# Copying queries and gates to the rounded type before their transposes, in both attention stages

## The chip, the cores and the metric

The kernel runs on one core of one Trainium2 chip. The metric is the device time of one execution in microseconds, and the kernel before takes 2444.26 us (median of three runs, 2442.14 to 2445.91). A core has five engines that the text speaks of: TensorE (PE in the profile, with its weight loads as PEld), VectorE (DVE), ScalarE (ACT), GpSimd (POOL) and SyncE (SP). SyncE only issues DMAs here; each engine works through its own instructions in order, and semaphores tie the engines together.

## The reference

One encoder layer is applied to two sequences of 2048 tokens with model width 1024. It normalises the input, projects it, attends in two head groups side by side, gates each group's output, projects back and adds a second gated input:

```
h = rms_norm(x);  proj = h @ w_in
q_a, k_a, v_a, g_a, q_b, k_b, v_b, g_b = split(proj)     # 512,128,128,512, 4 x 512
q_a, k_a: per-head rms_norm, partial rotary;  q_b, k_b: per-head rms_norm
o_a = windowed_gqa_sink(q_a, k_a, v_a, sink) * silu(g_a)  # 8 query heads, 2 kv heads, +-128 tokens
o_b = neighbourhood_attn(q_b, k_b, v_b, rpb) * silu(g_b)  # 8 heads, 2-D window on a grid 64 wide
x = x + concat(o_a, o_b) @ w_out
y = x + (p @ w_ple) * sigmoid(x @ w_ple_gate)
```

Everything is float32. The kernel keeps that precision with a rounded type (float32r, F32R in the code): a value is split into a rounded high part and the remainder, and each product is made of three products of rounded parts.

## The kernel before

**Stages.** The kernel goes through 96 blocks of 128 tokens, f = 0 to 95. The first 32 (two sequences of 16) are group A, where a block has two units, one for each kv head. The next 64 are group B, two halves of the heads with 32 blocks each, where a block is one unit. A last stage makes the output projections. In the attention stages the projections run ahead of the attention work of a unit as a stream of matmuls 512 columns wide, and the attention work of a unit is set into this stream at hand-written places: PLAN_A, PLAN_L (last unit of A), PLAN_B and PLAN_C are lists of (place in the unit, whether it is this unit's work or the previous unit's, action, index). The actions are scores (sc), exponentials (exp), in A the denominators (den), the transposes of the probabilities (pt), their products with the values (po), the preparation of the next block's queries (prep) and the end of the unit (fin). TensorE's order is pinned to the order in which the code emits its instructions (`pinned`); the other engines are ordered by the tile framework from dependencies and emission order, except where `P`, `behind` or `after` fixes a place.

**Transposes.** `tr` (lines 291 to 295) transposes a tile of 128 x 128 on TensorE with an identity: line 293 if the tile is of the rounded type, line 295 if it is plain float32. In group A's inner blocks, `turn` (line 736) copies a pair of probability tiles by a DMA on SyncE's queue, bits unchanged, to a tile of the rounded type, a ring of three places of 640 columns (`tna`), and line 293 transposes the copies. In the first and the last block of each sequence the probabilities are not copied and line 295 transposes them. In most of group B's units (`copied_`) the probabilities are copied in the same way by DMAs on ScalarE's queue (line 342).

**Queries.** In A, `prep_a` takes the block's queries (tile `qg`, 128 tokens by 8 heads of 64) from `held`, transposes them in a run of four as float32 into `pqt`, and `split_q` makes the high and low parts. In B, `prep_b` does so in a run of two into `pqtb`.

**Gates.** `exps` ends with GpSimd's product of the gate with the inverse denominators (line 359) into the tile `g2`, 256 columns, two buffers. `fin`, in the following unit, transposes it in a run of two as float32 into `pgt` or `pgtb`; VectorE multiplies it with the attention output (lines 809 and 1025), and SyncE stores the product (lines 810 and 1026).

**SyncE's queue** also carries the loads of inputs (`stx`, `stn`, line 393), the stores and loads of B's values (`v_d`, `vw`, lines 887 and 961), the bias loads (line 927) and the loads and stores of split weights (`wa`, `wb`, `sp_...`).

Of the kernel before, what the change touches and what calls it, by code (L numbers as in the profile page):

```python
# [11 lines left out]
F32 = mybir.dt.float32  # L12
F32R = mybir.dt.float32r
# [6 lines left out]
NT = SEQ // 128  # L20
KT = DM // 128
HD = 64
# [36 lines left out]
def bias_offsets():  # L59
# [32 lines left out]
KB = 23  # L92
PLAN_A = (
    (0.04, 1, "sc", 0), (0.08, 1, "sc", 1), (0.11, 1, "sc", 2), (0.12, 1, "rest", 0), (0.14, 1, "sc", 3),
    (0.14, 1, "rest", 1), (0.21, 0, "pt", 0), (0.26, 0, "pt", 1), (0.31, 0, "pt", 2),
    (0.32, 1, "exp", 0), (0.33, 1, "turn", 0), (0.33, 1, "turn", 1),
    (0.48, 0, "po", 0), (0.56, 0, "po", 1), (0.66, 1, "prep", 0), (0.66, 0, "po", 2), (0.74, 0, "fin", 0), (0.76, 1, "den", 0),
)
PLAN_L = tuple((part, now or act == "pt", act, i) for part, now, act, i in PLAN_A if act != "pt") + (
    (0.75, 1, "pt", 0), (0.79, 1, "pt", 1), (0.88, 1, "pt", 2),  # L100
# [1 line left out]
PLAN_B = (  # L102
    (0.00, 1, "sc", 0), (0.03, 1, "sc", 1), (0.07, 1, "sc", 2), (0.09, 0, "po", 2), (0.11, 1, "sc", 3), (0.16, 0, "po", 3),
    (0.16, 1, "exp", 0), (0.24, 0, "fin", 0), (0.35, 1, "prep", 0),
    (0.45, 1, "pt", 0), (0.52, 1, "pt", 1), (0.60, 1, "pt", 2), (0.66, 1, "po", 0), (0.74, 1, "pt", 3), (0.80, 1, "po", 1),
)
PLAN_C = (
    (0.00, 1, "sc", 0), (0.01, 0, "po", 0), (0.03, 1, "sc", 1), (0.05, 0, "po", 1), (0.07, 1, "sc", 2), (0.09, 0, "po", 2),
    (0.11, 1, "sc", 3), (0.16, 0, "po", 3), (0.16, 1, "exp", 0), (0.24, 0, "fin", 0), (0.35, 1, "prep", 0),
    (0.64, 1, "pt", 0), (0.73, 1, "pt", 1), (0.82, 1, "pt", 2), (0.91, 1, "pt", 3),  # L110
)


# [15 lines left out]
def emit(ctx, tc, io):  # L129
    nc = tc.nc  # L130
# [191 lines left out]
    def exps(sm, fct, gs, sink=None, turned=None):  # L322

        mx, nm, den, rd, ss = (sm[k] for k in ("mx", "nm", "den", "rd", "s"))
        if sink is None:
            nc.vector.tensor_scalar_mul(nm, mx, -1.0)  # L326
            yield
        else:
            nc.vector.scalar_tensor_tensor(out=nm, in0=mx, scalar=-1.0, in1=sink[1], op0=ALU.mult, op1=ALU.min)
            yield  # L330
        waiting = []
        for n_, i in enumerate((0, 2, 1, 3) if sink is None else range(4)):
            ex = nc.scalar.activation(ss[i], ss[i], AF.Exp, bias=nm[:, i:i + 1], accum_out=den[:, i:i + 1])  # L333
# [24 lines left out]
        g2 = ap.tile([128, 4, HD], F32, tag="g2", name="g2", bufs=2)  # L358
        nc.gpsimd.tensor_tensor(out=g2, in0=gs.rearrange("p (h d) -> p h d", h=4),
                                in1=rd.unsqueeze(2).broadcast_to([128, 4, HD]), op=ALU.mult)  # L360
        sm["g2"] = g2.rearrange("p h d -> p (h d)")
        yield

    def split_q(pqt, q1, q2, part):

# [339 lines left out]
    qrest = {}  # L705

    def prep_a(f):
        q = held[f][0]
        pqt = ptile([128, 512], "ms", "pqt")
        halves = pqt.rearrange("p (r x e q) -> p r e x q", r=2, x=2, e=2)  # L710
        for i in range(4):
            tr(halves[:, i // 2, i % 2], q[:, 2 * i:2 * i + 2, :].rearrange("p h d -> p (h d)"),
               ident.rearrange("p (x q) -> p x q", x=2))
        q1 = [ap.tile([128, 512], F32R, tag="q1", name="q1", bufs=3) for _ in range(2)]
        q2 = [q2s[f % 2][:, e] for e in range(2)]
        drain(split_q(pqt, q1, q2, 0))
        qrest[f] = split_q(pqt, q1, q2, 1)
        return q1, q2

    p_rot, s2, tn = [], [0, 0], []  # L720

    def unit_a(f, kv):
        s, t = divmod(f, NT)
# [5 lines left out]
        def turn(pair):  # L729

            if left and right:
                if len(s2) < 3:
                    s2.append(ap.tile([128, 3, 640], F32R, tag="ev", name="tna", bufs=1))
                to = s2[2][:, s2[1] % 3]
                s2[1] += 1
                nc.sync.dma_start(to.bitcast(F32), pairs[pair])
                pairs[pair] = to

# [57 lines left out]
        def fin(_):  # L796
# [9 lines left out]
            for e in range(2):  # L806
# [2 lines left out]
            nc.vector.tensor_tensor(out=ot, in0=pgt, in1=ot, op=ALU.mult)  # L809
            nc.sync.dma_start(oa_d[s].rearrange("(i p) q -> p i q", p=128)[:, 2 * kv:2 * kv + 2, 128 * t:128 * t + 128],  # L810
                              ot)
        return {"sc": sc, "turn": turn, "pt": pt, "po": po, "fin": fin, "prep": lambda _: nxt(f) if kv else None,
                "exp": lambda _: next(got["ex"]), "den": lambda _: next(got["ex"]), "rest": lambda _: None if kv else next(qrest[f])}

    pending = []
# [118 lines left out]
    def unit_b(f):  # L934
# [84 lines left out]
        def fin(_):  # L1019
            pgt = ptile([128, 2, 128], "sc", "pgtb")  # L1020
            for i in range(2):
# [5 lines left out]
        return {"sc": sc, "pt": pt, "po": po, "fin": fin, "prep": lambda _: nxt(f),  # L1027
                "exp": lambda _: (next(got["ex"]), ex_of.update({f: last_ex[-1]}), load_ahead(), load_values())}


# [500 lines left out]
```

## Time and profile before

| what | before |
|---|---|
| median of three runs | 2444.26 us (2442.14 to 2445.91) |
| profiled execution: its time | 2444.17 us |
| profiled execution: its span | 2442.4 us |
| granted TensorE clock | 1.00 |
| TensorE busy | 2428.9 us (99% of the span) |
| VectorE busy | 1739.9 us (71%) |
| ScalarE busy | 1423.1 us (58%) |
| GpSimd busy | 849.2 us (35%) |
| moved by DMAs | 516.38 MB, 211 GB/s in the mean |

The span is the time from the first to the last instruction in the profile. A row of the timeline gives the start, the length from the first start to the last end of the merged instructions, the engine, the line, what is written and read, and the number of instructions; in brackets is how long the engine stood idle before and what ended that. A row of a tile's view gives the shortest, median and longest duration in nanoseconds and the first and last start. A row of the windows' view ends with the granted clock, the share of the 16 DMA engines and GB/s.

### The profile page before, as it was taken

What the parts mean: (1) busy time and instruction counts of PE and PEld (TensorE: products, weight loads), DVE (VectorE), ACT (ScalarE), POOL (GpSimd) and SP (SyncE); (2) the same over time, 40 slices, a digit from 0 to 9 for tenths busy, and PEclk for the clock granted to TensorE, in tenths of its full rate; (3) what the DMA queues carried; (4) which work ended last, traced back from release to release, by engine and by line L of the source; (5) the groups of instructions that cost most, each with busy time, mean ns of one, the idle gap of its engine ahead of it and who ended that gap; (6) DMA issues with size and microseconds to landing.
All of it is one profiled execution on the core that took longest, in us unless ns stands there. A gap on an engine that the chain in (4) does not pass through costs nothing.

```text
span 2442.4 us, 41330 instructions
## 1 busy us (share of the span) xinstructions
PE 2428.9 (99%) x13062; PEld 2047.8 (84%) x13062; DVE 1739.9 (71%) x4215; ACT 1423.1 (58%) x3408; POOL 849.2 (35%) x1363
## 2 busy tenths in 40 slices
PE   9999999999999999999999999999999999999999
PEld 8888888888887888888888888888888888888887
DVE  7888888888875666666666677776537655677776
ACT  6777777777764666665666666666653222344443
POOL 5555555555543544454444444443100000000000
PEclk9999999999999999999999999999999999999999
DMA  6544443444464677767966677787887545855765
GB/s 235 186 155 158 155 148 115 160 156 157 149 234 142 214 240 249 234 211 260 305 224 226 221 261 258 248 272 258 297 280 244 171 149 186 270 182 204 250 223 171
DMA packets 291386, 516.38 MB, mean 211 GB/s; under 512 B 32960, under 2 KB 117856, under 8 KB 286944
## 3 DMA queue, kind: packets, MB, share of 16 engines
q1 hardware_dynamic: 261504, 474.55, 58.2%
q10 hardware_dynamic: 29664, 39.19, 5.3%
q8 instruction: 104, 1.70, 0.3%
q14 instruction: 114, 0.93, 0.1%
HBM read 307.72 MB, written 134.23 MB: 181 GB/s over the span
## 4 chain that ended last, share of the span: by engine, by line
PE 93%; DMA 3%; ACT 1%; DVE 1%; POOL 0%; issue 0%; SPq 0%; ACTq 0%; DVEq 0%; POOLq 0%
PE pqk L289 15%; PE pvg L289 14%; PE acca L1334 14%; PE accc L1334 11%; PE pg L289 7%; PE pq L289 7%; PE scb L289 3%; PE po L289 3%; PE pob L289 3%; PE sc L289 3%; PE pk L289 3%; PE pple L289 3%; PE ptb L293 2%; PE pt L293 2%; DMA vw<-v_d 1%; PE pktb L295 1%
## 5 line engine op out<-in xcount | busy, mean ns | idle before, releaser
L289 PE MATMUL pvg<-wb,xr 128*128 128x512 f32 x1536 | 471.2, 408 | 0.4 <-DMA wb<-sp_1wb 0.3
L289 PE MATMUL pqk<-wa,xr 128*128 128x512 f32 x1536 | 431.0, 408 | 0.0
L333 ACT ACTIVATE s<-s,nm 128x320 f32<-128x320 f32 (+6 forms) x512 | 294.8, 580 | 43.9 <-DVE nm L326 28.3
L289 PEld LDWEIGHTS pvg<-wb,xr 128*128 128x128 f32 x1536 | 273.0, 189 | 33.5 <-DMA wb<-sp_1wb 1.4
L289 PEld LDWEIGHTS pqk<-wa,xr 128*128 128x128 f32 x1536 | 264.9, 188 | 38.6
L1316 ACT CAST opd<-raw 128x512 fp32r<-128x512 f32 x224 | 131.5, 619 | 270.6 <-PE acca L1334 118.0
L411 POOL TENSOR_TENSOR xr<-stx,xr 128x512 fp32r<-128x512 f32 x186 | 237.8, 1294 | 104.5 <-ACT xr L410 66.4
L1317 DVE TENSOR_TENSOR opd<-raw,opd 128x512 fp32r<-128x512 f32 x224 | 146.6, 686 | 146.6 <-ACT opd L1316 146.6
L289 PE MATMUL pq<-wa,xr 128*128 128x512 f32 x768 | 241.3, 405 | 0.0
L289 PE MATMUL pg<-wb,xr 128*128 128x512 f32 x768 | 229.8, 405 | 0.9 <-DVE vv L568 0.9
L308 DVE CUSTOM_DVE_ANT_0 s<-scb,bias 128x288 f32<-128x288 f32 (+3 forms) x256 | 139.3, 548 | 71.2 <-PE scb L289 52.3
L1016 ACT COPY otb<-pob 64x512 f32<-64x512 f32 x128 | 74.5, 582 | 182.5 <-PE pob L289 181.9
L1334 PE MATMUL accc<-opd,wb 128*128 128x512 f32 x768 | 176.7, 389 | 0.0
L1334 PE MATMUL acca<-opd,wa 128*128 128x512 f32 (+1 forms) x780 | 175.9, 386 | 0.5 <-ACT r L1412 0.5
L1334 PE MATMUL acca<-opd,s 128*128 128x512 f32 x768 | 175.4, 389 | 0.0
L1334 PEld LDWEIGHTS acca<-opd,wa 128*128 128x128 f32 x780 | 145.0, 188 | 30.2 <-ACT r L1412 0.7
L1334 PEld LDWEIGHTS accc<-opd,wb 128*128 128x128 f32 x768 | 144.2, 188 | 29.9
L1334 PEld LDWEIGHTS acca<-opd,s 128*128 128x128 f32 x768 | 144.2, 188 | 29.9
L780 ACT CAST pr<-pt 128x512 fp32r<-128x512 f32 (+2 forms) x248 | 112.2, 474 | 86.5 <-PE pt L293 76.5
L174 POOL TENSOR_TENSOR yb<-vrb,power 128x8 f32<-128x8 f32 x64 | 106.3, 1661 | 145.5 <-DVE vrb L854 127.1
L289 PEld LDWEIGHTS pg<-wb,xr 128*128 128x128 f32 x768 | 135.6, 188 | 17.5 <-DVE vv L568 1.3
L289 PEld LDWEIGHTS pq<-wa,xr 128*128 128x128 f32 x768 | 132.6, 189 | 10.7
(192 smaller groups left out, 5169.1 us busy)
## 6 DMA issues: line engine op xcount, KB each, us to landing
tna<-s SPq DMA_DIRECT2D x112, 320.0 KB
stx<-x_b SPq DMA_DIRECT2D x128, 256.0 KB
vw<-v_d SPq DMA_DIRECT2D x96, 256.0 KB
v_d<-vb SPq DMA_DIRECT2D x64, 256.0 KB
xres<-x_r SPq DMA_DIRECT2D x64, 256.0 KB
raw<-x_d SPq DMA_DIRECT2D x16, 1024.0 KB
xres<-ple_d SPq DMA_DIRECT2D x64, 256.0 KB
xres<-x_d SPq DMA_DIRECT2D x64, 256.0 KB
```

The lines of the kernel that those rows point to most:

```text
L174: nc.gpsimd.tensor_tensor(out=y, in0=v, in1=power.broadcast_to([128, n]), op=ALU.pow)
L289: pinned(nc.tensor.matmul(out, lhsT, rhs, start=start, stop=stop))
L293: pinned(nc.tensor.transpose(out.bitcast(F32R), in_, eye))
L295: pinned(nc.tensor.transpose(out, in_, eye.bitcast(F32)))
L308: nc.vector.tensor_tensor_reduce(out=s, in0=ps[:, :n], in1=bias, scale=1.0, scalar=-3.0e38, op0=ALU.add, op1=ALU.max, accum_out=sm["mx"][: ...
L333: ex = nc.scalar.activation(ss[i], ss[i], AF.Exp, bias=nm[:, i:i + 1], accum_out=den[:, i:i + 1])
L411: low.tensor_tensor(out=lo, in0=raw, in1=hi.bitcast(F32), op=ALU.subtract)
L780: nc.scalar.copy(pr[r, 0, to], pt[r, c])
L1016: nc.scalar.copy(ot[a:a + 64], pq[z:z + 64])
L1316: P(nc.scalar.copy(hi, v))
L1317: P(nc.vector.tensor_tensor(out=lo, in0=v, in1=hi.bitcast(F32), op=ALU.subtract))
L1334: pinned(nc.tensor.matmul(ps[:, cols], w[k][:, a, c:c + 128], o[:, b, cols], start=i in (0, 1, 4) and k == 0 and j == 0, stop=k == 3 and j ...
```

## The change

Queries and gates are copied by DMAs on SyncE's queue, bits unchanged, to tiles of the rounded type, and line 293's form of the transpose takes the copies.

- A gate copy (`gcopy`, `turn_gate`) follows the gate's product in all units of both stages: at 0.77 of a unit of A, at 0.58 of a unit of B. `g2` has one buffer instead of two; the copy has one of its own, of the same size.
- In A, a query copy (`qcopy`, `turn_q`) at 0.30 of a block's first unit copies the next block's queries, for blocks 1 to 29, to columns 1280 to 1791 of `tna`. The ring of `tna` is now two fixed places, one for each pair of probabilities, beside these columns.
- In B, a query copy at 0.58 copies the queries of two units ahead, for units 34 to 95, to columns 384 to 511 of `q2s[1]`, which the units of B don't use otherwise.
- `prep_a` and `prep_b` transpose the copy where there is one, and the original otherwise.

```
+    (0.30, 1, "qcopy", 0)   and   (0.77, 1, "gcopy", 0)      in PLAN_A (and so in PLAN_L)
+    (0.58, 1, "qcopy", 0), (0.58, 1, "gcopy", 0)             in PLAN_B and PLAN_C

-        g2 = ap.tile([128, 4, HD], F32, tag="g2", name="g2", bufs=2)
+        g2 = ap.tile([128, 4, HD], F32, tag="g2", name="g2", bufs=1)

+    def turn_gate(sm):
+        g2r = ap.tile([128, 256], F32R, tag="g2r", name="g2r", bufs=1)
+        nc.sync.dma_start(g2r.bitcast(F32), sm["g2"])
+        sm["g2"] = g2r

     def prep_a(f):
-        q = held[f][0]
+        q = turned_q.get(f, held[f][0])

+    def turned_a():
+        if not tna:
+            tna.append(ap.tile([128, 1920], F32R, tag="ev", name="tna", bufs=1))
+        return tna[0]
+
+    def turn_q(f):
+        if f < 2 * NT:
+            to, q = turned_a()[:, 1280:1792].rearrange("p (h d) -> p h d", d=HD), held[f][0]
+            nc.sync.dma_start(to.bitcast(F32), q)
+        else:
+            to = q2s[1][:, :, 384:512]
+            nc.sync.dma_start(to.bitcast(F32), held[f][0].rearrange("p (i h) d -> p i (h d)", i=2))
+        turned_q[f] = to

             if left and right:
-                if len(s2) < 3:
-                    s2.append(ap.tile([128, 3, 640], F32R, tag="ev", name="tna", bufs=1))
-                to = s2[2][:, s2[1] % 3]
-                s2[1] += 1
+                to = turned_a()[:, 640 * pair:640 * pair + 640]
                 nc.sync.dma_start(to.bitcast(F32), pairs[pair])
...
+    unit_a:  "gcopy": lambda _: turn_gate(sm),
+             "qcopy": lambda _: turn_q(f + 1) if kv == 0 and f + 1 < 2 * NT - 2 else None
...
     def prep_b(f):
-        q = held[f][0]
+        q = turned_q.get(f, held[f][0].rearrange("p (i h) d -> p i (h d)", i=2))
         for i in range(2):
-            tr(pqt[:, 128 * i:128 * i + 128], q[:, 2 * i:2 * i + 2, :].rearrange("p h d -> p (h d)"))
+            tr(pqt[:, 128 * i:128 * i + 128], q[:, i])
...
+    unit_b:  "gcopy": lambda _: turn_gate(sm),
+             "qcopy": lambda _: turn_q(f + 2) if f + 2 < 6 * NT else None
```

More of the change, by code (lines that the diff above doesn't have):

```diff
@@ L94 @@
     (0.04, 1, "sc", 0), (0.08, 1, "sc", 1), (0.11, 1, "sc", 2), (0.12, 1, "rest", 0), (0.14, 1, "sc", 3),
-    (0.14, 1, "rest", 1), (0.21, 0, "pt", 0), (0.26, 0, "pt", 1), (0.31, 0, "pt", 2),
+    (0.14, 1, "rest", 1), (0.21, 0, "pt", 0), (0.26, 0, "pt", 1), (0.30, 1, "qcopy", 0), (0.31, 0, "pt", 2),
     (0.32, 1, "exp", 0), (0.33, 1, "turn", 0), (0.33, 1, "turn", 1),
     (0.48, 0, "po", 0), (0.56, 0, "po", 1), (0.66, 1, "prep", 0), (0.66, 0, "po", 2), (0.74, 0, "fin", 0), (0.76, 1, "den", 0),
+    (0.77, 1, "gcopy", 0),
 )
@@ L104 @@
     (0.16, 1, "exp", 0), (0.24, 0, "fin", 0), (0.35, 1, "prep", 0),
-    (0.45, 1, "pt", 0), (0.52, 1, "pt", 1), (0.60, 1, "pt", 2), (0.66, 1, "po", 0), (0.74, 1, "pt", 3), (0.80, 1, "po", 1),
+    (0.45, 1, "pt", 0), (0.52, 1, "pt", 1), (0.58, 1, "qcopy", 0), (0.58, 1, "gcopy", 0), (0.60, 1, "pt", 2), (0.66, 1, "po", 0), (0.74, 1, "pt", 3), (0.80, 1, "po", 1),
 )
@@ L109 @@
     (0.11, 1, "sc", 3), (0.16, 0, "po", 3), (0.16, 1, "exp", 0), (0.24, 0, "fin", 0), (0.35, 1, "prep", 0),
-    (0.64, 1, "pt", 0), (0.73, 1, "pt", 1), (0.82, 1, "pt", 2), (0.91, 1, "pt", 3),
+    (0.58, 1, "qcopy", 0), (0.58, 1, "gcopy", 0), (0.64, 1, "pt", 0), (0.73, 1, "pt", 1), (0.82, 1, "pt", 2), (0.91, 1, "pt", 3),
 )
@@ L718, in prep_a @@
         return q1, q2
-    p_rot, s2, tn = [], [0, 0], []
+    p_rot, s2, tn, tna, turned_q = [], [0], [], [], {}
+    def turned_a():
[10 more added lines that the diff above has]
+        turned_q[f] = to
     def unit_a(f, kv):
@@ L811, in fin @@
                               ot)
-        return {"sc": sc, "turn": turn, "pt": pt, "po": po, "fin": fin, "prep": lambda _: nxt(f) if kv else None,
+        return {"sc": sc, "turn": turn, "gcopy": lambda _: turn_gate(sm),
+                "qcopy": lambda _: turn_q(f + 1) if kv == 0 and f + 1 < 2 * NT - 2 else None, "pt": pt, "po": po, "fin": fin, "prep": lambda _: nxt(f) if kv else None,
                 "exp": lambda _: next(got["ex"]), "den": lambda _: next(got["ex"]), "rest": lambda _: None if kv else next(qrest[f])}
@@ L1026, in fin @@
             nc.sync.dma_start(ob_d[s][b, :, 2 * half:2 * half + 2, cb, :], o_t)
-        return {"sc": sc, "pt": pt, "po": po, "fin": fin, "prep": lambda _: nxt(f),
+        return {"sc": sc, "pt": pt, "po": po, "fin": fin, "prep": lambda _: nxt(f), "gcopy": lambda _: turn_gate(sm),
+                "qcopy": lambda _: turn_q(f + 2) if f + 2 < 6 * NT else None,
                 "exp": lambda _: (next(got["ex"]), ex_of.update({f: last_ex[-1]}), load_ahead(), load_values())}
```

## Prediction

> **What bounds the kernel now.** I read the page's totals first, then the four tiles whose transposes change, then the timeline of TensorE around one transpose of each type, then the SyncE, GpSimd and TensorE rows around the places where a copy would have to land.
>
> ```profile
> span 2442.4 us, 41330 instructions
> ...
> PE 2428.9 (99%) x13062; PEld 2047.8 (84%) x13062; DVE 1739.9 (71%) x4215; ACT 1423.1 (58%) x3408; POOL 849.2 (35%) x1363
> ...
> PE 93%; DMA 3%; ACT 1%; DVE 1%; POOL 0%; issue 0%; SPq 0%; ACTq 0%; DVEq 0%; POOLq 0%
> ```
>
> TensorE is busy for 99% of the span and makes 93% of the chain of waits. A nanosecond taken from its stream is a nanosecond of the kernel, unless it has to wait for what replaces it. So two sums are needed: what the transposes give back, and where TensorE would wait for a copy.
>
> ```profile
> L295 PE MATMUL pgt<-ident,g x128: 270/272/327, 55.2 to 745.4; 128*128 128x128 f32 x128
> ...
> L295 PE MATMUL pqt<-ident,q x128: 270/272/328, 34.1 to 720.2; 128*128 128x128 f32 x128
> ...
> L295 PE MATMUL pqtb<-ident,qg x128: 270/272/275, 738.8 to 1774.3; 128*128 128x128 f32 x128
> ...
> L295 PE MATMUL pgtb<-rowwise,g x128: 270/272/298, 809.8 to 1793.9; 128*128 128x128 f32 x128
> ...
> L293 PE MATMUL pt<-ident,tna 128*128 128x128 f32 x560 | 67.3, 235 | 0.0
> ```
>
> Each of the four tiles has 128 transposes of 272 ns as plain float32 (line 295). The copied probabilities, transposed as the rounded type (line 293), take 235 ns. The plain product would be 37 ns times 496 changed transposes, 18 us. That is not the gain: these durations overlap their neighbours, and only the distance from start to start counts.
>
> **The change part by part. The transposes.** The kernel already holds both types in the same pattern of work: the first and last block of each sequence leave the probabilities as float32. The timeline of TensorE there:
>
> ```profile
> 413.49 0.38 PE L295 MATMUL pt<-ident,s 128*128 128x128 f32 x2
> 413.62 0.71 PE L289 MATMUL pq<-wa,xr 128*128 128x512 f32 x2
> 414.17 0.60 PE L295 MATMUL pt<-ident,s 128*128 128x128 f32 x4
> 414.53 1.40 PE L289 MATMUL pq<-wa,xr 128*128 128x512 f32 x5
> 415.77 0.40 PE L289 MATMUL po<-pr,vv 128*128 128x256 f32 x2
> ```
>
> and in an inner block, rounded type:
>
> ```profile
> 645.97 0.29 PE L293 MATMUL pt<-ident,tna 128*128 128x128 f32 x2
> 646.10 0.70 PE L289 MATMUL pg<-wb,xr 128*128 128x512 f32 x2
> 646.64 0.45 PE L293 MATMUL pt<-ident,tna 128*128 128x128 f32 x4
> 646.93 0.47 PE L289 MATMUL pg<-wb,xr 128*128 128x512 f32 x1
> 647.24 0.46 PE L293 MATMUL pt<-ident,tna 128*128 128x128 f32 x4
> 647.53 1.39 PE L289 MATMUL pg<-wb,xr 128*128 128x512 f32 x5
> 648.75 0.64 PE L289 MATMUL po<-pr,vv 128*128 128x256 f32 x4
> ```
>
> Four transposes and five projections: 415.77 - 414.17 = 1.60 us as float32, 648.75 - 647.24 = 1.51 us rounded. I take 0.08 us for a run of four (0.09 less a row's rounding). Two transposes and two projections: 414.17 - 413.49 = 0.68 us against 646.64 - 645.97 = 0.67 us. A pair gives 0.01 by these rows. Their ends are rounded to 0.01 us each, and a quarter of 0.08 per transpose would give 0.04, so a pair lies between 0.01 and 0.03. I take 0.02, because a pair keeps the switch to and from the projections, where the rounded type wins least.
>
> Counts from the code: group A's queries are turned in runs of four, for blocks 1 to 29 (29 runs). Gates go in pairs, 64 in A and 64 in B; B's queries in pairs, 62 units (the first two aren't copied). 29 x 0.08 + 190 x 0.02 = 2.3 + 3.8 = **6.1 us given back**, bounds 29 x 0.08 + 190 x 0.01 = 4.2 and 29 x 0.08 + 190 x 0.03 = 8.0. The wait on a DMA's semaphore is in this price already: the transposes of line 293 have it too.
>
> **The copies: when they are ready, and when they are needed.** 128 gate copies and 91 query copies are added to SyncE's queue. In group A:
>
> ```profile
> 413.27 0.61 POOL L359 TENSOR_TENSOR g<-gs,rd 128x256 f32<-128x256 f32 x1
> ...
> 412.21 0.33 SPq L393 DMA_DIRECT2D stn<-x_n  x1
> 415.43 0.53 SPq L736 DMA_DIRECT2D tna<-s  x1
> ...
> 418.54 0.38 PE L295 MATMUL pgt<-ident,g 128*128 128x128 f32 x2
> ...
> SPq L736 <- ACT s L333: 220.8, 55, 5.0
> ```
>
> The gate is ready at 413.88, SyncE has nothing to issue from 412.54 to 415.43, and TensorE takes the gate at 418.54, 4.66 us later. What does a copy take?
>
> ```profile
> 363.02 1.56 SPq L736 DMA_DIRECT2D tna<-s  x2
> ...
> 365.60 0.15 POOL L748 MEMSET s<- 128x64 f32 x1 [2.57 <-DMA tna<-s]
> ...
> q1 hardware_dynamic: 261504, 474.55, 58.2%
> ```
>
> A copy inside SBUF of 320 KB, issued at 363.02, releases GpSimd by 365.60: 2.6 us, an upper bound for 128 KB. The queue row gives 58.2% of 2442 us for 474.55 MB, 3.0 us a MB, so 0.19 MB less is 0.6 us less: 2.0 us. I take 2.1, between 2.0 and 2.6. With 4.66 us of cover, this is hidden; the other unit of a block starts from a gate that is ready earlier still. If the gate copy waits at the head of SyncE's queue, behind it are the next squares' loads (stn) and the probabilities' copies (tna). The tna issue at 415.43 comes after the gate's readiness in any case, and it waits for ScalarE's exponentials (the last row: 220.8 us of SyncE's waits), not for the queue. Queries are issued at 0.30 of a block's first unit and read at 0.66 of its second, 0.68 of a block of (720.2 - 34.1)/31 = 22.1 us: 15 us of cover. The probabilities' ring of three places becomes two fixed ones. Their copies wait for the exponentials of the unit, which follow the previous unit's last transposes, so I cost that at nothing; without this cover a copy would start some tenths of a us later, of several us that it has.
>
> In group B:
>
> ```profile
> 1096.14 1.42 SPq L961 DMA_DIRECT2D vw<-v_d  x3
> 1097.65 0.45 SPq L927 DMA_DIRECT2D bias<-bias  x1
> ...
> 1096.81 0.61 POOL L359 TENSOR_TENSOR g<-qg,rd 128x256 f32<-128x256 f32 x1
> ...
> 1109.27 0.38 PE L295 MATMUL pgtb<-rowwise,g 128*128 128x128 f32 x2
> ```
>
> Gate ready at 1097.42, read at 1109.27: 11.9 us. One buffer instead of two for the gate's product makes the next product wait for the previous copy, a whole unit of (1793.9 - 809.8)/63 = 15.6 us earlier. B's queries are copied two units ahead from tiles that are ready long before. All hidden.
>
> **The seam.** One gate has no cover. After the last unit of group A, its values' product and its gate follow at once:
>
> ```profile
> 742.17 5.25 SPq L810 DMA_DIRECT2D oa_d<-ot  x2
> ...
> 744.61 0.61 POOL L359 TENSOR_TENSOR g<-gs,rd 128x256 f32<-128x256 f32 x1
> ...
> 745.27 0.44 PE L295 MATMUL pgt<-ident,g 128*128 128x128 f32 x2 [0.46 <-POOL g L359]
> ```
>
> TensorE already waits there for GpSimd, until 745.27. Now the copy comes between: 745.22 + 2.1 = 747.3. The queue is idle at that time (the second store of line 810 itself waits for this transpose), so **2.1 us are lost**, once, with the next block's projections queued behind the waiting transpose on TensorE, and VectorE's product (line 809) and its store after it. Bounds 2.0 and 2.6.
>
> **The traffic.** 190 copies of 0.131 MB and 29 of 0.262 MB are 32.5 MB, at 3.0 us a MB 97 us of the 16 engines, 4% of the span and 0.8 us a unit of B. That matters where the engines are full and TensorE already waits for a load:
>
> ```profile
> 1205.00:1210.00 5.00, 5.00 (x29) 4.04 (x27) 2.84 (x10) 2.53 (x6) 2.04 (x2) 1.00 1.02 402
> ...
> 1720.00:1725.00 5.00, 3.80 (x21) 2.73 (x20) 3.37 (x8) 4.63 (x11) 1.71 (x4) 1.00 1.06 333
> ...
> PE pob L289 <- DMA vw<-v_d: 1.6, 4, 0.9
> PE pvg L289 <- DMA wb<-sp_1wb: 0.3, 1, 0.3
> ```
>
> The DMA share is 1.02 and 1.06 in two stretches (the column before the last), where weights of the second half and, late in B, values come late. At each, up to one unit's copies lie ahead of the late load: 0 to 0.8 us each, 0 to 1.6 in sum. I take 0.6, nearer to nothing, because a copy issued before the stretch is done by then.
>
> **Sum:** -6.1 + 2.1 + 0.6 = -3.4 us. The profiled execution has a span of 2442.4 and took 2444.17, so 1.8 us lie around the span; 2439.0 + 1.8 = 2440.8. The median of the runs, 2444.26, is 0.1 above: **2440.9 us**.
>
> **The rivals.** *The whole gain, cover everywhere (faster).* The pairs give 0.02 to 0.03, the seam's gate is ready earlier in another order of VectorE's work, and the full stretches absorb the traffic: 2444.3 - 6.1 = 2438.2, down to 2436.3. For it: the seam is one place of 128. Against: TensorE waits for GpSimd there already.
>
> *Nothing gained from the type.* A float32 transpose already streams as fast as a rounded one, and the 37 ns are latency. Then only seam and traffic stay: 2444.3 + 2.7 = 2447.0. Against it are the starts: four in 0.60 us with a last one of 0.272 are (0.60 - 0.27)/3 = 0.11 us apart, rounded (0.45 - 0.235)/3 = 0.07. [...]
>
> *SyncE's order (slower).* If the gate copy of A's second units is placed behind the two tna copies, it issues at about 417.5 instead of 413.9 and lands at 417.5 + 2.1 = 419.6, where TensorE wants it at 418.54: 1.1 us in each of 32 units, 35 us, less the 3.4: 2476. It decides as soon as the copy is issued after 416.4. Against it: the plan puts it (0.77) ahead of the next unit's copies (0.33).
>
> *Late B (slower).* If each of the last nine units' values come later by the two copies' issue (0.4 us each, as the bias row's 0.45) and their 0.8 us of traffic, and TensorE waits for all of it, 9 x 1.6 = 14 us: 2455. It decides when the values land after their product's turn. For it: the 0.9 us wait. Against: one wait in 1.2 us or less a unit is all that shows now.
>
> **How the numbers follow.** Chances: forecast 0.50, whole gain 0.31, nothing gained 0.05, late B 0.09, SyncE's order 0.05. A measurement of this kernel tells a change from none at about 0.2%, 4.9 us. The forecast (-3.4) and nothing gained (+2.7) lie within it: 0.55. Whole gain is faster: 0.31. The last two are slower: 0.14. The range runs from 2436.5, the whole gain at its best, to 2447.5, nothing gained with the seam at 2.6; what is left out is the two slower rivals and a little of either side.
>
> **What would show it.** Right: the four tiles' transposes on line 293's kind at about 235 ns; runs of two and two projections at 0.66 to 0.67 us; one wait of TensorE of about 2 us at the end of group A, ended by a DMA; gate copies issued right behind GpSimd's product. Wrong: TensorE waiting for the gate copy in inner units, waits for vw or wb that add up to more than 4 us, or starts of float32 and rounded pairs that don't differ.

## The result, and the profile after

The kernel after takes 2467.08 us (median of 6 runs, 2463.75 to 2472.04), the kernel before beside it 2444.31 us. The ratio is 1.0093, 95% interval 1.008 to 1.0106: 22.8 us slower, where 3.4 us faster was forecast. The profiled execution took 2466.75 us, with a span of 2465.0. Medians here and below are over all executions of a run; a single one of 4547.87 us, in the last run but two, is left out of that run's ratio.

The page's totals, chain of waits and SyncE's queue, after:

```profile
span 2465.0 us, 41869 instructions
...
PE 2430.2 (99%) x13062; PEld 2041.5 (83%) x13062; DVE 1733.7 (70%) x4215; ACT 1420.9 (58%) x3408; POOL 847.1 (34%) x1363
...
q1 hardware_dynamic: 300976, 507.07, 61.5%
...
PE 76%; DMA 7%; ACT 7%; DVE 6%; issue 2%; SPq 1%; POOL 1%; ACTq 0%; DVEq 0%; POOLq 0%
```

TensorE is still busy for 99%, but its share of the chain fell from 93% to 76%; DMAs, ScalarE and VectorE now make 20% of it. The queue moves the 32.5 MB more that were forecast.

The transposes became shorter, as forecast. TensorE's timeline around one block's queries (pqt) and gate (pgt), before:

```profile
428.76 0.60 PE L295 MATMUL pqt<-ident,q 128*128 128x128 f32 x4
429.12 0.72 PE L289 MATMUL pk<-wx,xr 128*128 128x256 f32 x4
429.67 0.38 PE L295 MATMUL pgt<-ident,g 128*128 128x128 f32 x2
```

and after:

```profile
429.61 0.46 PE L294 MATMUL pqt<-ident,tna 128*128 128x128 f32 x4
429.91 0.70 PE L290 MATMUL pk<-wx,xr 128*128 128x256 f32 x4
430.45 0.29 PE L294 MATMUL pgt<-ident,g2r 128*128 128x128 f32 x2
```

Four query transposes and four projections take 429.67 - 428.76 = 0.91 us before and 430.45 - 429.61 = 0.84 after. From the first transpose's start to that of the second matmul behind the run, the median difference over all runs of four is 0.074 us, over all pairs 0.024: 29 x 0.074 + 190 x 0.024 = 6.7 us, against 6.1 forecast.

So 22.8 + 6.7 = 29.5 us were lost elsewhere. Where, is read from the **lag**: the start of VectorE's product with a unit's gate (the instruction that reads pgt or pgtb) after, minus the start of the same unit's product before. Columns are the times of that product in the kernel before, and a lag is from one profiled execution of each kernel:

| run | 57 us | 677 | 742 | 811 | 1177 | 1228 | 1464 | 1702 | 1797 |
|---|---|---|---|---|---|---|---|---|---|
| after | +1.4 | +0.5 | +2.6 | +6.0 | +10.0 | +16.0 | +16.0 | +19.9 | +22.0 |

Group A (to 747) gains 0.9 us between 57 and 677; the lag then jumps at its end, around 1200, and in many small steps in group B. The waits that TensorE has now and didn't have before (its view of waits: total us, times, longest):

```profile
PE pgtb L294 <- DMA g2r<-g: 5.8, 2, 5.2
PE scb L290 <- DVE mx L309: 4.8, 7, 1.2
PE pgt L294 <- DMA g2r<-g: 3.2, 2, 2.6
```

and VectorE's wait for the bias tiles of group B, before and then after:

```profile
DVE s L308 <- DMA bias<-bias: 15.8, 12, 2.6
```

```profile
DVE s L309 <- DMA bias<-bias: 45.7, 21, 3.8
```

The gate copies (g2r) that TensorE waits for are four of 128. The longest, on GpSimd, SyncE and TensorE:

```profile
1205.38 0.61 POOL L360 TENSOR_TENSOR g<-qg,rd 128x256 f32<-128x256 f32 x1
```

```profile
1204.97 1.00 SPq L229 DMA_DIRECT2D wb<-sp_1wb  x2
1208.76 1.20 SPq L908 DMA_DIRECT2D v_d<-vb  x2
1210.06 4.88 SPq L229 DMA_DIRECT2D wb<-sp_1wb  x6
1215.00 0.72 SPq L742 DMA_DIRECT2D q<-qg  x1
1215.81 0.65 SPq L368 DMA_DIRECT2D g2r<-g  x1
```

```profile
1217.84 1.24 PE L290 MATMUL pvg<-wb,xr 128*128 128x512 f32 x4
1224.23 0.47 PE L294 MATMUL pgtb<-rowwise,g2r 128*128 128x128 f32 x2 [5.16 <-DMA g2r<-g]
1224.50 2.46 PE L290 MATMUL pvg<-wb,xr 128*128 128x512 f32 x5
1226.76 0.41 PE L294 MATMUL pqtb<-ident,q 128*128 128x128 f32 x2
```

The gate was ready at 1205.99. Two weight loads of 512 KB (wb) had just been issued; ahead of the copy SyncE still had two stores of values (v_d), which it issued only at 1208.76, six more weight loads and a query copy, and it came to the gate's copy at 1215.81. The DMA engines were full then (shares 0.98 and 1.04, rows in the last section), and TensorE got the copy at 1224.23, 8.4 us after its issue, not 2.1.

The other kind is an order. SyncE in the middle of group B, after, and the two ends of what its last row delays, on VectorE and TensorE:

```profile
981.91 0.66 SPq L742 DMA_DIRECT2D q<-qg  x1
982.66 1.52 SPq L982 DMA_DIRECT2D vw<-v_d  x3
984.27 0.50 SPq L368 DMA_DIRECT2D g2r<-g  x1
984.87 0.55 SPq L948 DMA_DIRECT2D bias<-bias  x1
```

```profile
991.43 0.46 DVE L309 CUSTOM_DVE_ANT_0 s<-scb,bias 128x288 f32<-128x288 f32 x1 [3.25 <-DMA bias<-bias]
```

```profile
991.95 0.40 PE L290 MATMUL scb<-ks_b,q1b 128*128 128x288 f32 x1 [0.50 <-DVE mx L309]
```

Both copies stand ahead of the next unit's bias. VectorE waits 3.25 us for it, the softmax starts late, and TensorE waits 0.50 us for a free scores' tile.

### The profile page after: what moved, and what is told of

Read it like the earlier page. It is cut to its first block, busy times and chain, and to the rows that moved or that the text cites. A ratio compares the mean times of both kernels' runs of the same rounds, so it can differ in the third digit from the quotient of the medians.

```text
span 2465.0 us, 41869 instructions
## 1 busy us (share of the span) xinstructions
PE 2430.2 (99%) x13062; PEld 2041.5 (83%) x13062; DVE 1733.7 (70%) x4215; ACT 1420.9 (58%) x3408; POOL 847.1 (34%) x1363
## 4 chain that ended last, share of the span: by engine, by line
PE 76%; DMA 7%; ACT 7%; DVE 6%; issue 2%; SPq 1%; POOL 1%; ACTq 0%; DVEq 0%; POOLq 0%
PE acca L1356 14%; PE pvg L290 13%; PE pqk L290 12%; PE accc L1356 10%; PE pq L290 6%; PE pg L290 5%; PE scb L290 3%; PE pob L290 3%; PE pple L290 2%; PE sc L290 2%; ACT s L334 2%; PE po L290 2%; PE pt L294 2%; PE ptb L294 1%; DMA vw<-v_d 1%
## 5 line engine op out<-in xcount | busy, mean ns | idle before, releaser
L309 DVE CUSTOM_DVE_ANT_0 s<-scb,bias 128x288 f32<-128x288 f32 (+3 forms) x256 | 137.7, 546 | 105.0 <-DMA bias<-bias 45.7
```

The lines of the kernel that those rows point to most:

```text
L309: nc.vector.tensor_tensor_reduce(out=s, in0=ps[:, :n], in1=bias, scale=1.0, scalar=-3.0e38, op0=ALU.add, op1=ALU.max, accum_out=sm["mx"][: ...
```

## The experiments

What a run lost or gained is told against the kernel before in the runs beside it (2443.33 us for the first four, then 2443.0, 2443.21 and 2442.57 for each four).

**Which half of the change, and is the type worth it at all?** Four runs: the type without copies, the copies of one group each, and copies that nobody reads.

```diff
-g2 = ap.tile([128, 4, HD], F32, tag="g2", name="g2", bufs=2)
+g2 = ap.tile([128, 4, HD], F32R, tag="g2", name="g2", bufs=2)
...
-q = ap.tile([128, 8, HD], F32, tag="qg", name="q", bufs=6)
+q = ap.tile([128, 8, HD], F32R, tag="qg", name="q", bufs=6)
...
-qg = ap.tile([128, 2, 4, HD], F32, tag="qg", name="qg", bufs=6)
+qg = ap.tile([128, 2, 4, HD], F32R, tag="qg", name="qg", bufs=6)
```

> No copy at all: the kernel before, with the query tile, the query and gate tile of group B and the gate tile g2 declared as the rounded type, so that VectorE, GpSimd and ScalarE round them as they write, and the transposes run as that type. Queries and gates are thereby rounded, which the kernel before doesn't do, so the outputs change. Theory (late landings: the type pays, the copies cost): only the gain is left, at most 190 x 0.024 + 29 x 0.074 = 6.7 us, less what VectorE's chain takes back in group A; 2438 to 2442 us, no gate wait, no longer bias waits than before. Rival (the type gains nothing on the path): 2443 to 2446 us. In group A the period of 22.13 us per two units should fall by about 0.03 if VectorE sets it, by 0.12 if TensorE does.

Measured: 2442.22 us, ratio 0.9991 (0.9982 to 1.0). Without copies the type is no loss, but of 6.7 us only 1.1 is left, and the interval reaches 1.0.

```diff
-(0.58, 1, "qcopy", 0), (0.58, 1, "gcopy", 0),
```

> The copies of group A alone; group B transposes the original queries and gates, with two gate tiles as before. Theory (late landings): the A copies are to blame for what was lost up to the first units of B, +6.0 us at 811 us (+1.4 in the first block, -0.85 over 28 blocks, +2.1 between 660 and 742, +3.4 at the end of group A), and nothing after it: 2448 to 2451 us. Rival (traffic spread over both stages in proportion to the bytes): about half of 22.8 us, 2455 us, lost evenly over the blocks of A.

Measured: 2451.13 us, ratio 1.0029 (1.0017 to 1.0041): 7.8 us lost, just above the theory's range. By place the theory holds only in part: its lag is +3.0 at 811 us, not +6.0, and +3.2 at 1702, and the last 2.5 us come after that, where this run has no copies. Why is open. Of the 3.0 that are missing at 811, 1.3 are missing from 742 on: the wait at the end of group A is as long as in after, but the eight projections behind it took 2.10 us, not 3.29 (last section).

```diff
-(0.30, 1, "qcopy", 0),
...
-(0.77, 1, "gcopy", 0),
```

> The copies of group B alone; group A as before, three places in its ring and two gate tiles. Theory (late landings): +16 us, in steps: two late gate copies at about 1185 and 1220 us (5.8 us of waits and some 1.4 of clock after them) and about ten units in which VectorE waits 3 to 4 us for a bias tile issued behind the copies; 2458 to 2462 us, VectorE's waits for bias some 45 us against 15.8 before. Rival (traffic): 2455 us, with no such steps.

Measured: 2464.39 us, ratio 1.0083 (1.007 to 1.0097): 21.1 us lost, more than the theory said, and with group A's 7.8 more than both together cost. VectorE waits 59.9 us for bias in this profile (of the slowest execution, 2470.63 us), against 45.7 in after. Why more bias tiles come late here isn't settled.

```diff
-    def turn_gate(sm):
+    def turn_gate(sm, in_b):
-        g2r = ap.tile([128, 256], F32R, tag="g2r", name="g2r", bufs=1)
-        nc.sync.dma_start(g2r.bitcast(F32), sm["g2"])
-        sm["g2"] = g2r
+        to = ap.tile([128, 256], F32R, tag="g2r", name="g2r", bufs=1) if in_b else turned_a()[:, 1280:1536]
+        nc.sync.dma_start(to.bitcast(F32), sm["g2"])
...
-        turned_q[f] = to
```

> All the copies are made as in the kernel after, but nobody reads them: the transposes take the originals in full FP32. So the copies' issue and bytes stay, and TensorE never waits for their landing. Theory (late landings, half of it at the gates and half through the bias): 2467 less 9.0 us of gate waits and 2.7 us of clock after them, plus the 6.7 us that the type gained: 2458 to 2466 us, VectorE's bias waits still about 45 us. Rival 1 (issue, order and bytes alone): nothing goes away but the gain, 2470 to 2477 us. Rival 2 (the landing at the transposes is all of it): 2443 to 2448 us plus at most the 6.7.

Measured: 2452.05 us, ratio 1.003 (1.002 to 1.004): 8.7 us lost, less than the theory said, and within the second rival's bound. So the bytes themselves are not the 22.8 us. But the run changed more than it was meant to: its edit also gave group A its second gate tile back and put that group's gate copies into `tna`, and the order changed. SyncE in group B of this run:

```profile
1051.08 1.43 SPq L983 DMA_DIRECT2D vw<-v_d  x3
1052.60 0.51 SPq L371 DMA_DIRECT2D g2r<-g  x1
1053.20 0.54 SPq L949 DMA_DIRECT2D bias<-bias  x1
1054.38 1.91 SPq L909 DMA_DIRECT2D v_d<-vb  x3
1060.05 0.66 SPq L744 DMA_DIRECT2D q<-qg  x1
```

With no reader the query copy was scheduled behind the bias, and VectorE's waits for bias are 23.1 us, not 45.7. That made a new theory: the order of SyncE, apart from the landing.

**The order and the late gates, one at a time.** The order first, with both copies behind the bias:

```diff
+            if bias_loads:
+                behind(copy, bias_loads[-1])
...
             if 6 * NT - 9 <= f < 6 * NT - 1:
                 load_bias(f + 1, P)
+            elif 2 * NT < f < 6 * NT - 9:
+                load_bias(f + 1)
...
+"exp": lambda _: (..., load_values(), load_ahead()) if 2 * NT < f < 6 * NT - 9 else
```

> The kernel after with one order changed on SyncE in group B (but for its last nine units): the next unit's bias tile is loaded right behind the unit's values, and the copies of query and gate behind it, where after has them ahead of it. Theory (SyncE's order: two copies push the bias back by 1.2 to 2 us, VectorE starts the softmax late, TensorE waits for the scores' tile): VectorE's waits for bias fall from 45.7 to some 20 us and the run comes out about 10 us below after, 2455 to 2460 us, with the late gates at 1185 and 1224 us still there. Rival (the bias waits are off the path, the gates' landing is all): 2464 to 2469 us. Against the theory speaks that the gate copy now stands behind 960 KB more, of a slack of 6.3 us in the middle.

Measured: 2466.34 us, ratio 1.0092 (1.0079 to 1.0105), 23.3 us lost: the rival's number, yet not its reason. TensorE's waits for gates in this run:

```profile
PE pgtb L294 <- DMA g2r<-g: 8.9, 6, 4.3
PE pgt L294 <- DMA g2r<-g: 3.4, 2, 2.6
```

VectorE's waits for bias fell to 22.3 us, as the theory said. But the gate copy now stands behind a bias of up to 960 KB and three stores, and TensorE waits for it in six units instead of two. The loss changed its place.

```diff
-"gcopy": lambda _: turn_gate(sm),
+"gcopy": lambda _: turn_gate(sm) if (f, kv) not in ((29, 1), (31, 1)) else None,
 "qcopy": lambda _: turn_q(f + 1) if kv == 0 and f + 1 < 2 * NT - 2 else None,
...
-"gcopy": lambda _: turn_gate(sm),
+"gcopy": lambda _: turn_gate(sm) if f not in (55, 57) else None,
 "qcopy": lambda _: turn_q(f + 2) if f + 2 < 6 * NT else None,
```

> The kernel after without four of its 128 gate copies, those that TensorE was seen to wait for (the second half of blocks 29 and 31 of group A, the units 55 and 57 of group B, whose copies stand behind the weights of the next stage or at the end of group A): these four gates are transposed from the originals in full FP32. Theory (landing behind a full queue): 5.8 + 3.2 us of waits and 2.7 us of slower matmuls after them go away, 4 x 0.024 us of gain with them: 2454 to 2458 us. Rival (the time is only spent in the next wait): 2463 to 2467 us.

Measured: 2463.54 us, ratio 1.0078 (1.0066 to 1.009): 20.5 us lost, 2.3 less than after and not 9 to 13, and the intervals overlap. The lag shows both halves of it: it is +2.0 at 811 us (+6.0 after) and rises by 2.4 from 1177 to 1228 (6.0 after), so 7.6 us went away where the gates had been late. But VectorE waits 58.2 us for bias here, and the lag rises by 5.3 from 811 to 1177 (4.0 after) and by 6.1 from 1702 to 1797 (2.1). At 1219 a query copy behind the same weights is waited for instead (2.2 us).

Then both edits together.

> The last two together: bias ahead of the copies, and four gates from the originals. Theory: what both lose is all but the gains taken back in group A and the first block: 2442 to 2448 us, no further from the kernel before than the run with the types rounded at the source (2442.2) and 5 us more. Rival (a third cost, the bytes or SyncE's time themselves): 2450 us or more.

Measured: 2459.92 us, ratio 1.0066 (1.0054 to 1.0078): 16.9 us lost. That is the rival's range, and the theory, that these two are all, falls in this form: six gate waits of 6.2 us in sum and one of 2.5 us for a query are left, made by the order with the bias first.

```diff
-    def turn_gate(sm):
+    def turn_gate(sm, queue=nc.sync):
...
-        nc.sync.dma_start(g2r.bitcast(F32), sm["g2"])
+        queue.dma_start(g2r.bitcast(F32), sm["g2"])
...
-            nc.sync.dma_start(to.bitcast(F32), held[f][0].rearrange("p (i h) d -> p i (h d)", i=2))
+            nc.scalar.dma_start(to.bitcast(F32), held[f][0].rearrange("p (i h) d -> p i (h d)", i=2))
...
-"gcopy": lambda _: turn_gate(sm),
+"gcopy": lambda _: turn_gate(sm, nc.scalar),
 "qcopy": lambda _: turn_q(f + 2) if f + 2 < 6 * NT else None,
```

> The kernel after with the copies of group B issued by ScalarE on its own queue (group A's stay with SyncE). Theory (what costs is the place in SyncE's order, not the bytes): the bias is issued as before, no gate stands behind SyncE's weight loads; the A copies' loss stays (2451.1 with the A copies alone), and ScalarE pays 128 issues of some 0.5 us and their waits, in part on the path: 2450 to 2456 us. Rival (bytes: 97 us of 16 engines wherever they are issued): 2463 us or more. ScalarE as the new bound, waiting in order for GpSimd's gate, would show as TensorE's waits for ScalarE's copies, 2460 us or more.

Measured: 2457.78 us, ratio 1.0061 (1.0049 to 1.0073): 14.8 us lost, 1.8 us above the theory's range. The bytes are the same, yet 8.0 us came back: VectorE's waits for bias are 19.6 us, and TensorE waits for no gate in group B. Beside group A's part, what is left in group B has another name in its waits, that of the weight loads:

```profile
PEld ptb L294 <- DVE p_t L1019: 10.5, 15, 2.0
```

ScalarE issues 126 DMAs more. As I read this row, the high parts that it writes of the transposed probabilities (line 1018) come later for that, VectorE's low parts (line 1019) behind them, and TensorE waits there; that was not tried. Taking group B's copies out of SyncE's order and queue was worth 8.0 us.

Then the order that the unread copies had shown, values, gate, bias, query:

```diff
-(0.58, 1, "qcopy", 0), (0.58, 1, "gcopy", 0),
+(0.58, 1, "gcopy", 0), (0.58, 1, "bias", 0), (0.58, 1, "qcopy", 0),
...
+            if bias_loads:
+                behind(copy, bias_loads[-1])
...
+"bias": lambda _: load_bias(f + 1) if 2 * NT < f < 6 * NT - 9 else None,
```

> The kernel after with SyncE's order in group B (but for its last nine units) set to: the unit's values, its gate copy, the next unit's bias tile, and the query copy last, which is read some 10 us later and can wait. What the run with both copies behind the bias showed (VectorE's bias waits 45.7 to 22.3 us, but TensorE waiting 8.9 us for gates that then landed late) would be avoided: the gate gives way to nothing, the bias to the gate alone. Theory (SyncE's single queue has room for one copy ahead of the bias but not for two): bias waits 20 to 28 us, gate waits as in after (9 us), 2456 to 2461 us. Rival (any copy ahead of the bias or behind it costs the same): 2464 to 2468 us.

Measured: 2458.74 us, ratio 1.0061 (1.0047 to 1.0074), in the theory's range: 15.5 us lost, 7.3 less than after. VectorE's waits for bias fell less than the theory said, to 33.5 us and not to 20 to 28:

```profile
DVE s L309 <- DMA bias<-bias: 33.5, 21, 3.0
```

But TensorE's wait for VectorE behind a late bias (`PE scb <- DVE mx`, 4.8 us in after) is gone from its view. The lag rises by 1.0 us from 811 to 1177 (4.0 after) and falls by 1.0 from 1228 to 1702 (rises by 3.9 after). The steps at the end of group A and around 1200 are still there, as they must be. In the profiled execution, the slowest of this run (2463.13 us), the lag also rises by 5.8 from 1702 to 1797 (2.1 after), in the last units, whose order is not changed. With this order kept, the late places were left out too:

```diff
-"gcopy": lambda _: turn_gate(sm),
+"gcopy": lambda _: turn_gate(sm) if f > 2 and (f, kv) not in ((29, 1), (31, 1)) else None,
-"qcopy": lambda _: turn_q(f + 1) if kv == 0 and f + 1 < 2 * NT - 2 else None,
+"qcopy": lambda _: turn_q(f + 1) if kv == 0 and f > 2 and f + 1 < 2 * NT - 2 else None,
...
-"gcopy": lambda _: turn_gate(sm),
+"gcopy": lambda _: turn_gate(sm) if f not in (55, 56, 57) and f < 6 * NT - 9 else None,
-"qcopy": lambda _: turn_q(f + 2) if f + 2 < 6 * NT else None,
+"qcopy": lambda _: turn_q(f + 2) if f not in (55, 56, 57) and f + 2 < 6 * NT - 9 else None,
```

> The last order, and no copies where they were late: none in the first three blocks of group A, none of the gate in the second half of its blocks 29 and 31, none in group B's units 55 to 57 (beside the weights of the second half) and its last nine; there the originals are transposed in full FP32. Theory (the losses are at these places and in the order of SyncE): what is left of them is small and group A's gain is mostly VectorE's, 2443 to 2449 us. Rival (a third cost, spread over group B): 2452 us or more.

Measured: 2447.48 us, ratio 1.0017 (1.0008 to 1.0026), as the theory said. With the order mended and the late places left out, 18.5 of the 22.8 us are gone. The rest is still a loss of 4.3 us: no version with copies that was run paid. VectorE still waits 38.1 us for bias here, in 21 waits, while 22.3 us of such waits stood beside a loss of 23.3 us with both copies behind the bias. So the sum of VectorE's waits does not measure the loss; it costs where TensorE comes to wait for VectorE (scb, 4.8 us in after, 1.4 here). Of the rest, 2.5 us of lag arise between 677 and 742 us, where TensorE waits for no gate; why is open.

**Who takes group A's gain?** There, with copies or without, hardly any copy was late, and still the lag moved by only 0.9 to 1.1 us between 57 and 677 us. In the views of waits for 100 to 655 us, TensorE's weight loads wait for VectorE before, after, and with the types rounded at the source:

```profile
PEld sc L289 <- DVE mx L308: 8.2, 24, 0.6
```

```profile
PEld sc L290 <- DVE mx L309: 10.8, 25, 0.6
```

```profile
PEld sc L289 <- DVE mx L308: 10.3, 25, 0.6
```

The third score of a block needs a tile that VectorE's softmax frees. A faster TensorE gets there earlier and waits longer. If so, a shorter VectorE must release the gain. One instruction was left out of it, in both bases, the addition of the sink's term to the denominators, which cost in group A before (100 to 650 us):

```profile
L350 DVE TENSOR_TENSOR den<-den,es 128x4 f32<-128x4 f32 x50 | 26.1, 521 | 0.8
```

```diff
-behind(nc.vector.tensor_tensor(out=den, in0=den, in1=es, op=ALU.add))
-nc.vector.reciprocal(out=nm, in_=den)
+behind(nc.vector.reciprocal(out=nm, in_=den))
```

> Types rounded at the source, no copies, as in the first of these runs (2442.2 us), and VectorE relieved of one instruction in each unit of group A: the sink's term is left out of the denominators (the addition of es to den, 520 ns of VectorE), so group A's outputs change. Theory (VectorE's chain sets group A, so TensorE's shorter transposes come back as waits for VectorE: 8.4 us of TensorE's stalls there against 3.2 before): the gain now appears, the stalls fall by about 5 us, 2436 to 2440 us. Rival (VectorE isn't what takes it): 2441 to 2443 us.

Measured: 2430.61 us, ratio 0.9946 (0.9934 to 0.9959): 12.6 us gained, better than the theory's range.

> The kernel before with the same instruction left out (the sink's term isn't added to group A's denominators): the base for the run before this one. With the slow transposes TensorE has only 3.2 us of stalls in group A, so the relief alone can bring at most that: 2440 to 2443 us. Theory (VectorE takes the transposes' gain): the type is worth 3 us or more with the relief against 1 us without. Rival: it is worth the same 1 us in both.

Measured: 2436.1 us, ratio 0.9968 (0.9955 to 0.998). The relief alone brought 7.1 us, more than the bound that I had put on it; I had counted only TensorE's longer stalls, not the 8.2 us of short waits of its weight loads. With the relief the type is worth 2436.1 - 2430.6 = 5.5 us, without it 2443.3 - 2442.2 = 1.1. In group A alone, from 57 to 677 us, the lag falls by 7.4 us with the relief and by 11.1 with relief and type: 3.7 more. The windows' view of group A (busy us of TensorE, weight loads, VectorE, ScalarE, GpSimd), rounded at the source without and with the relief:

```profile
100.00:655.00 555.00, 553.02 (x3421) 480.20 (x3420) 463.40 (x1357) 409.69 (x1126) 299.08 (x634) 1.00 0.45 150
```

```profile
100.00:655.00 555.00, 555.00 (x3477) 488.67 (x3477) 448.27 (x1329) 416.15 (x1148) 305.74 (x651) 1.00 0.46 154
```

With the relief TensorE has no pause left and does 3477 instead of 3421 matmuls in the same 555 us. The waits of weight loads for VectorE's softmax (sc <- DVE mx, 24 to 25 of them above) are gone from that stretch in both runs with the relief. VectorE, busy for 463 of 555 us (83%), had set the pace.

**The same with no work left out, and the two copies apart.**

```diff
-behind(nc.vector.tensor_tensor(out=den, in0=den, in1=es, op=ALU.add))
-nc.vector.reciprocal(out=nm, in_=den)
+nc.gpsimd.tensor_tensor(out=den, in0=den, in1=es, op=ALU.add)
+behind(nc.vector.reciprocal(out=nm, in_=den))
```

> Types rounded at the source, no copies (2442.2 us), and the addition of es to den in group A done by GpSimd instead of VectorE: nothing of the computation is left out but the rounding of queries and gates that this base has. With the addition left out altogether the same base took 2430.6 us. Theory (VectorE's instructions and its waits set group A): most of that 11.6 us comes, if GpSimd's result is there when VectorE takes its reciprocal: 2431 to 2437 us. Rival (VectorE then waits for GpSimd, whose rope instructions stand ahead of the addition): 2440 us or more.

Measured: 2431.54 us, ratio 0.9955 (0.9942 to 0.9967): 11.0 us gained.

> The kernel before with the same addition moved to GpSimd and nothing else: exact as before. Theory: near the 2436.1 us that it took with the addition left out, 2436 to 2440 us. Rival (VectorE waits for GpSimd): 2443 us or more.

Measured: 2436.7 us, ratio 0.9975 (0.9965 to 0.9984). Both as the theory said. The second computes what the kernel before computes, with one addition on another engine, and is 0.25% faster than it; the first rounds queries and gates as well, and is 0.45% faster.

```diff
-(0.30, 1, "qcopy", 0),
...
-(0.58, 1, "qcopy", 0), (0.58, 1, "gcopy", 0),
+(0.58, 1, "gcopy", 0),
```

> The kernel after without the copies of queries: only the gates go by SyncE and are transposed as the rounded type, in both groups. Theory (late gates at four places, 9 us of waits and 2.7 of clock, and one copy ahead of the bias instead of two): 2455 to 2460 us, VectorE's bias waits 25 to 35 us. Rival (two halves alike, by their bytes): 2455 us less the gain, and the queries' run the same.

Measured: 2454.24 us, ratio 1.0045 (1.0033 to 1.0058), VectorE's waits for bias 23.3 us. Of the gates' 11.7 us, 9.3 lie where the gates landed late: the lag rises from -0.8 at 677 us to +4.9 at 811, and from +4.0 to +7.6 around 1200; elsewhere it falls or stands, but for 2.4 us after 1702. Time and waits are both just below the theory's ranges.

```diff
-(0.77, 1, "gcopy", 0),
...
-(0.58, 1, "qcopy", 0), (0.58, 1, "gcopy", 0),
+(0.58, 1, "qcopy", 0),
```

> The kernel after without the copies of gates (two gate tiles as before): only the queries go by SyncE. Theory (queries have some 10 us until they are read, but in group B one more copy stands ahead of the bias, and one lands late beside the weights of the second half): 2446 to 2452 us, VectorE's bias waits 25 to 35 us. Rival (two halves alike, by their bytes): 2455 us.

Measured: 2451.03 us, ratio 1.0031 (1.002 to 1.0041), waits for bias 35.6 us. The queries cost 8.5 us: 1.0 in the first block, the rest in group B. The two halves sum to 20.1 of 22.8 us.

## Why the prediction was wrong

**The transposes** were right: 6.7 us from the starts, 6.1 forecast. The rival that nothing is gained from the type is refuted. Here four float32 transposes take 429.12 - 428.76 = 0.36 us to the next matmul and four rounded ones 429.91 - 429.61 = 0.30.

**What bounds the kernel** was the first step that failed: "A nanosecond taken from its stream is a nanosecond of the kernel, unless it has to wait for what replaces it". TensorE was busy for 99%, but in group A VectorE set the pace, and its sign stood in the profile of before as 24 short waits of weight loads, 8.2 us in 555. Of group A's gain, 29 x 0.074 + 64 x 0.024 = 3.7 us, the lag kept about 1. With VectorE relieved 3.7 came.

**"All hidden"** was the step that cost most, in two ways. For the copies' own time I took 2.1 us, from a copy on a queue with nothing ahead; beside the weights of the second half it was 8.4 us, after 9.8 us in which the gate was ready and SyncE had other DMAs to issue ahead of it: 18.2 us, where TensorE, which then waited 5.16 us, came for the gate after 13.1 (11.9 in the forecast). And I asked when the copies would be late, but not who stands behind them: the fence of group B showed the bias load right behind the values, and I did not look up when VectorE takes it. The profile of before had the answer, 12 waits of 15.8 us in sum. A load without slack was pushed back by two issues and two transfers, to 21 waits and 45.7 us, and TensorE came to wait behind them. Moving the query copy behind the bias brought 7.3 us.

**The seam** had the right place and mechanism: TensorE waited there for a DMA. The copy was issued at 747.87 and TensorE had it at 750.01, 2.1 us later, as forecast:

```profile
747.87 0.53 SPq L368 DMA_DIRECT2D g2r<-g  x1
```

The wait of 2.57 us is these 2.1 on top of 0.46 that were there before. Mis-sized was what follows: the lag rises by 3.4 us from 742 to 811, 2.1 for the wait and the rest behind it, where eight projections took 3.29 us beside a granted clock of 0.50 (last section).

**The traffic** as bytes was forecast at 0.6 us. The runs bound it from above: with all bytes moved and none read, and the order changed, 8.7 us are left; with the same bytes on two queues, 8.0 us less than after. How much of it is bytes alone stays open.

**The rivals.** "SyncE's order" was the right kind of mechanism in the wrong group: in group A two gate copies of 64 were waited for, and not through the probabilities' copies; in group B the order did cost, on the bias, by the 7.3 us above. "Late B" named values; TensorE's waits for values stayed at 1.3 us. "The whole gain" needs a relieved VectorE and no copies: that run is 5.2 to 5.5 us below its own base. The signs listed as wrong appeared: TensorE waiting for the gate copy in inner units. The slower side had 0.14.

**Open** are the 1.0 us that query copies cost in group A's first block, what the last version with copies still loses, and why group B alone lost more than in the whole change. Copies in the mended order together with a relieved VectorE were not run, so whether copies can pay then isn't shown.

## What to carry to other kernels

Before a DMA is added to a queue, look up for every load behind it when its reader takes it, and who waits for that reader: a load that is already waited for can pass on the issues and bytes put ahead of it (VectorE's waits for bias were 15.8 us before and 45.7 after). Price a copy's landing by what is queued ahead at that place, not by a copy on an idle queue (8.4 us beside the weights against 2.1). And TensorE's share of 99% busy didn't mean here that it set the pace: 24 short waits of its weight loads for VectorE, 8.2 us in 555 of group A, were the sign that what was gained on it would be waited away. Leaving out one instruction of VectorE tested it: 7.1 us gained.

## What the runs showed of the hardware

Behind two of TensorE's waits in after its matmuls took longer too. In the windows' view of after (the columns end with granted clock, DMA share and GB/s), the long wait before 1224.23 and the stretch behind it, then the stretch behind the wait at the end of group A:

```profile
1219.10:1224.20 5.10, 0.00 (x0) 0.00 (x0) 0.87 (x2) 2.51 (x7) 1.02 (x2) 0.98 1.04 392
1224.30:1226.90 2.60, 2.60 (x9) 2.01 (x9) 1.09 (x3) 0.00 (x0) 0.55 (x1) 0.50 0.91 254
750.10:752.60 2.50, 2.50 (x8) 2.02 (x9) 0.42 (x1) 0.00 (x0) 0.00 (x0) 0.50 0.20 56
```

The share of the DMA engines was 0.98 from 1214 to 1219. The granted clock is 0.50 for about 2.5 us behind both waits. Behind the first, five projections took 1226.76 - 1224.50 = 2.26 us to the next matmul; the same five in the kernel before:

```profile
1208.31 1.41 PE L289 MATMUL pvg<-wb,xr 128*128 128x512 f32 x5
1209.56 0.38 PE L295 MATMUL pqtb<-ident,qg 128*128 128x128 f32 x2
```

1.25 us, with the granted clock at 1.00 from 1208.2 to 1209.6: 1.0 us less. The wait at the end of group A, in after and in the run with group A's copies alone:

```profile
750.01 0.47 PE L294 MATMUL pgt<-ident,g2r 128*128 128x128 f32 x2 [2.57 <-DMA g2r<-g]
750.28 3.29 PE L290 MATMUL pvg<-wb,xr 128*128 128x512 f32 x8
```

```profile
748.25 0.33 PE L294 MATMUL pgt<-ident,g2r 128*128 128x128 f32 x2 [2.57 <-DMA g2r<-g]
748.42 2.10 PE L290 MATMUL pvg<-wb,xr 128*128 128x512 f32 x8
```

The wait is the same, 2.57 us, but in the second run the same eight projections took 2.10 us and not 3.29, 1.2 us less. What decides is not tried here.

The addition of four numbers a partition, in the view of tile den of the kernel before (shortest, median and longest ns, first and last start), and one of the long ones on VectorE, with GpSimd at that time:

```profile
L350 DVE TENSOR_TENSOR den<-den,es x64: 144/165/1109, 44.5 to 742.6; 128x4 f32<-128x4 f32 x64
```

```profile
410.07 0.88 DVE L350 TENSOR_TENSOR den<-den,es 128x4 f32<-128x4 f32 x1
409.64 2.54 POOL L411 TENSOR_TENSOR xr<-stx,xr 128x512 fp32r<-128x512 f32 x2
```

It takes 144 to 165 ns in 35 units and 867 to 1109 ns in the other 29. In each of these 29 it starts while the first of a pair of GpSimd's subtractions of line 411 (1.3 us each) is running, and ends within 0.02 us of that one's end; in none of the 35 is line 411 running. So it is held up until GpSimd's instruction is done; that is read from the trace, not tried by moving line 411. Leaving the addition out or moving it brought 5.9 to 7.1 us in the kernel before.
